# Result rows added to a residual by accumulating DMAs instead of loads, VectorE sums and identity products

## The chip, the cores and the metric

One core of a Trainium2 chip. The metric is the time of one execution on the device, in microseconds (us).

## The reference

Two layers over 512 tokens of width 1024, in float32. Layer 0 mixes tokens by sparse attention, layer 1 by gated linear attention (GLA); both have memory heads beside. Every layer ends with a mixture of 32 experts, of which each token uses two, and two layer norms:

```python
x = layer_norm(ALPHA * x + mixed, ln1_g[i], ln1_b[i])
ffn = hier_moe(x, ...)          # two experts per token, weighted and summed
x = layer_norm(ALPHA * x + ffn, ln2_g[i], ln2_b[i])
```

The change touches the last line: the residual `ALPHA * x` plus the rows that the experts gave, then the norm.

## The kernel before

The 512 tokens lie in four row tiles of 128 rows by 1024 columns, `xb[0]` to `xb[3]`. After the mixer the kernel gathers each expert's tokens (at most 64) and works through the experts in nine groups (`GROUPS`, L1069): seven of four experts and two of two. `moe` (L1191) computes for each group the hidden products (`hidden`, L1096, matmuls at L1103), turns the result (`turned`, L1110) and multiplies by the output weights (L1266), two experts at a time in the two halves of the partitions.

Where the results go depends on the group. Groups 0 to 6 (28 experts) scale their rows into `ys` (L1274) and scatter them to a buffer `Y` in HBM (L1282, an indirect DMA on POOL). `Y` has two halves of 512 rows: a token's row from its first expert is in the first half, that from its second in the second. Both halves are cleared beforehand. The last two groups (experts 28 to 31) are local: their rows are split into a high and a low part `yh`, `yl` (L1270, L1271) and brought to their tokens by products with a one-hot matrix `sp` (L1257). `spread` holds these triples, one for each of the two pairs.

The weights stream in through one DMA queue, issued by SP in a planned order (`load_weights`, L1073, issue at L1055). They go to blocks of an arena in SBUF: `Arena.get` takes the least recently freed place, and a load waits until the former readers of that place are done. Pieces are of 2048, 1536, 1024 or 512 columns, as room is found. Behind layer 0's weights the weights of the GLA layer follow (`split_later`, L309, issue at L312, split by L295 on ScalarE and L296 on VectorE).

At the start of the last group `read_back` (L1355) takes four arena blocks `yb` and issues four loads of `Y` on SP, 1 MB each: row tile i of both halves. The engines' order from there on is the order of the code (`in_order`, L259). `add_first` (L1365) adds the first half of tiles 0 and 1 to the residual on VectorE. `combine` (L1369) ends the layer:

- `part(i, n, early)` brings tile i together in two PSUM tiles of 512 columns. For the first pair (n = 0) it begins with products of `yb` and the identity matrix (L1386): for tiles 0 and 1 of the second half alone, for tiles 2 and 3 of both halves. Then come the one-hot products of `yh` and `yl` (L1388).
- `add(i)` adds PSUM to the residual and forms the sums for the mean (L1395, L1399); ScalarE squares (L1401) and takes the root (L1402).
- `norm(i)` scales and shifts on VectorE (L1407 to L1409).
- `done(i, x)` stores the tile. In layer 1 this is the output (L1743), in layer 0 the store to `x2d` (L1749) and the transposes for the GLA layer's input (`fill`, L1434, L1439).

```python
part(0, 0, True)
part(1, 0, True)
for i in range(NT):
    part(i, 1, False)
    add(i)
    if i + 2 < NT:
        part(i + 2, 0, True)
    if i:
        norm(i - 1)
```

The PSUM pools `mm` and `sc` have two buffers each, so two row tiles are under way at a time. Then the GLA layer begins with its projection (`in_proj`, L558, products at L340 to L342).

Of the kernel before, what the change touches and what calls it, by code (L numbers as in the profile page):

```python
# [10 lines left out]
F32 = mybir.dt.float32  # L11
# [4 lines left out]
OP = mybir.AluOpType  # L16
AX = mybir.AxisListType

P = 128
S = 512  # L20
NT = S // P
D = 1024
# [206 lines left out]
class Trunk:  # L229
# [961 lines left out]
    def moe(self, layer, xb, Y, done):  # L1191


        nc, wk, ar = self.nc, self.wk, self.ar
        NQ = NE // QE
        W = QE * CAP
        xs = [b.v(D) for b in self.xs.blocks]
        xe = [b.v(KD // 2, W)[:, k] for b in self.xe.blocks for k in range(KD // 2)]
        scat, spread, held = [], [], []
        place = {}  # L1200
        oh, ins = self.one_hot(0)
        self.fetch(self.slot_tokens(oh), xs)
        ovf = self.overflow_count()
        with self.tc.issue_after(ins.ins):
            self.routing_rows()
        then = self.slot_tokens(self.one_hot(1)[0])
        self.overflow(layer, Y, ovf)
        order = self.pe_order()
        order.__enter__()
        self.features(xs, xe)  # L1210
        self.fetch(then, xs)
        for g, experts in enumerate(self.GROUPS):
            q, n = experts[0] // QE, len(experts)
            last = g == len(self.GROUPS) - 1
            turns = experts[-1] % QE == QE - 1 and q + 1 < NQ
            if g == NQ - 4:
                self.load_norms(layer)
            if last:
                self.read_back(Y)
                tail = self.in_order((mybir.EngineType.PE, mybir.EngineType.DVE, mybir.EngineType.Activation))  # L1220
                tail.__enter__()
            sas = []
            for s, e in enumerate(experts):
                blocks, rows = self.loaded.pop((layer, e, 0))
                sas.append(self.hidden(xe, e % QE, rows.__getitem__))
                for blk in blocks:
                    blk.free()
                if not last:
                    self.prefetch(layer, *((2 * D,) if g in (NQ - 3, NQ - 2) else ()))
                if g == 0 and s in (1, 2):  # L1230
                    place[s - 1] = self.places(s - 1, self.one_hot(s - 1)[0])
            if turns:
                self.features(xs, xe)
            aT = self.turned(sas)
            if turns and q + 2 < NQ:
                oh, _ = self.one_hot(q + 2)
                place[q + 2] = self.places(q + 2, oh)
                self.fetch(place[q + 2][0], xs)
            if g == NQ - 3:
                self.residual(xb, self.spread_norm(0, ALPHA))  # L1240
            if g == NQ - 2:
                self.gain = self.spread_norm(2, 1.0)
                self.rows.free()
            if last:
                self.xe.free()
                self.xs.free()
            _, token, wt, row = place[q]
            for s in range(0, n, 2):
                j = experts[s] % QE // 2
                ws = [self.loaded.pop((layer, e, 1)) for e in experts[s:s + 2]]  # L1250
                local = q == NQ - 1
                if local:
                    yb = (ar.get(D), ar.get(D))
                    yh, yl = (b.v(D, dt=F32R) for b in yb)
                    ohb = ar.get(S)
                    sp = ohb.v(S, dt=F32R)
                    nc.vector.tensor_scalar(sp, self.c("iota"), token[:, j:j + 1], None, op0=OP.is_equal)  # L1257
                    if last:
                        self.add_first(xb, 0)
                else:  # L1260
                    ys = wk.tile([P, D], F32, name="ys", tag="ys")
                for c in range(2):
                    y = self.pv([P, 512])
                    for f in range(2):
                        for h in range(2):
                            nc.tensor.matmul(y[h * CAP:(h + 1) * CAP, :], aT[:, s + h, f * CAP:(f + 1) * CAP],  # L1266
                                             ws[h][1][2 * f + c], start=(f == 0), stop=(f == 1))
                    cs = slice(c * 512, (c + 1) * 512)
                    if local:
                        nc.scalar.activation(yh[:, cs], y, AF.Copy, scale=wt[:, j:j + 1])  # L1270
                        nc.vector.scalar_tensor_tensor(yl[:, cs], y, wt[:, j:j + 1], yh[:, cs].bitcast(F32),  # L1271
                                                       op0=OP.mult, op1=OP.subtract)
                    else:
                        nc.scalar.activation(ys[:, cs], y, AF.Copy, scale=wt[:, j:j + 1])  # L1274
                for blocks, _ in ws:
                    for blk in blocks:
                        blk.free()
                if local:
                    spread.append((sp, yh, yl))
                    held.extend((ohb, *yb))  # L1280
                    continue
                st = nc.gpsimd.indirect_dma_start(  # L1282
                    out=Y, out_offset=bass.IndirectOffsetOnAxis(ap=row[:, j:j + 1], axis=0),
                    in_=ys, in_offset=None, bounds_check=2 * S - 1, oob_is_err=False)
                for b in scat:
                    self.tc.declare_no_dep(st.ins, b.ins, reason="rows of other slots")
                scat.append(st)
            if not last:
                self.prefetch(layer, *{NQ - 5: (D,), NQ - 4: (2 * D,), NQ - 3: (2 * D,), NQ - 2: (D, D, S)}.get(g, ()))
        self.add_first(xb, 1)  # L1290
        self.combine(xb, spread, done)
        tail.__exit__(None, None, None)
        order.__exit__(None, None, None)
        for b in held:
            b.free()
# [56 lines left out]
                out=Y, out_offset=bass.IndirectOffsetOnAxis(ap=idx[:, 0:1], axis=0),  # L1352
                in_=ys[:CAP], in_offset=None, bounds_check=2 * S - 1, oob_is_err=False)

    def read_back(self, Y):  # L1355

        yv = Y.rearrange("(r i p) f -> p r i f", r=2, p=P)
        self.yb = [self.ar.get(2 * D) for _ in range(NT)]
        for i in range(NT):
            self.nc.sync.dma_start(self.yb[i].v(2, D), yv[:, :, i, :])  # L1360


    EARLY = 2

    def add_first(self, hb, i):  # L1365
        x = hb[i].v(D)
        self.nc.vector.tensor_add(x, x, self.yb[i].v(2, D)[:, 0, :])

    def combine(self, hb, spread, done):  # L1369


        nc, ar, sm = self.nc, self.ar, self.sm
        g, b = (self.gain.v(2, D)[:, j] for j in range(2))
        sqb = ar.get(D)
        st, acc = {}, {}
        last = len(spread) - 1

        def part(i, n, early):

            oh, yh, yl = spread[n]  # L1380
            for c in range(2):
                cs = slice(c * 512, (c + 1) * 512)
                if early:
                    ps = acc[i, c] = (self.mm if c else self.sc)([P, 512])
                    for r in range(int(i < self.EARLY), 2):
                        nc.tensor.matmul(ps, self.ident, self.yb[i].v(2, D)[:, r, cs], start=(r == int(i < self.EARLY)), stop=False)  # L1386
                for y in (yh, yl):
                    nc.tensor.matmul(acc[i, c], oh[:, i * P:(i + 1) * P], y[:, cs], start=False, stop=not early and y is yl)  # L1388

        def add(i):  # L1390
            x = hb[i].v(D)
            s = sm.tile([P, 2], F32, name="csum")
            for c in range(2):
                cs = slice(c * 512, (c + 1) * 512)
                nc.vector.scalar_tensor_tensor(x[:, cs], acc[i, c], 1.0, x[:, cs], op0=OP.mult, op1=OP.add,  # L1395
                                               accum_out=s[:, c:c + 1])
            self.yb[i].free()
            nm = sm.tile([P, 1], F32, name="cmean")
            nc.vector.tensor_scalar(nm, s[:, 0:1], s[:, 1:2], -1.0 / D, op0=OP.add, op1=OP.mult)  # L1399
            sq = sm.tile([P, 1], F32, name="csq")  # L1400
            nc.scalar.activation(sqb.v(D), x, AF.Square, bias=nm, accum_out=sq)  # L1401
            nc.scalar.activation(sq, sq, AF.Sqrt, bias=self.eps[:, 0:1], scale=1.0 / D)  # L1402
            st[i] = x, nm, sq

        def norm(i):
# [3 lines left out]
            nc.vector.scalar_tensor_tensor(x, x, sq, b, op0=OP.mult, op1=OP.add)  # L1409
# [5 lines that stand above are left out]
# [394 lines left out]
```

## Time and profile before

| | us |
|---|---|
| median of 3 runs | 1210.11 |
| lowest, highest | 1205.82, 1212.65 |
| the profiled execution's own time | 1212.06 |
| its span in the profile | 1210.3 |
| TensorE busy | 1105.9 |
| VectorE busy | 591.2 |
| ScalarE busy | 398.5 |
| POOL busy | 178.8 |

Times in the rows are from the start of the span. The stages of layer 0 reach to about 660 us, the last 270 us are the MoE stage of layer 1. A busy share says where an engine works, not what ends last; for that there are the chain of waits, which is followed back from the last instruction, and the timeline, which gives in brackets how long an engine was idle before an instruction and what ended it. PEclk is the granted clock of TensorE as a share of full speed. "HBM" rows and GB/s are those of the core's 16 DMA engines together.

### The profile page before, as it was taken

To read this page: it belongs to the slowest core of one execution; us is meant where nothing else is said; L and a number is where in the kernel's file an instruction comes from. 1 tells how busy PE (TensorE), PEld (TensorE's weight loads), DVE (VectorE), ACT (ScalarE), POOL (GpSimd) and SP (SyncE) were. 2 spreads that over 40 slices of the span, in tenths; PEclk is the share of its full clock that TensorE was granted. 3 is DMA by queue.
4 is the path that set the end of the run, shared out by engine and by line. 5 is a ranking of instruction groups with operands and counts; after the bars stand their busy time and mean duration, and the time that the engine had idled before them with its cause. 6 is when DMAs were issued, how large, how long until landed. Compare 5 with 4: busy or idle time off the path is not lost. (4 is left out here: it accounts for less than half of the span.)

```text
span 1210.3 us, 20344 instructions
## 1 busy us (share of the span) xinstructions
PE 1105.9 (91%) x7864; PEld 799.5 (66%) x7864; DVE 591.2 (49%) x1601; ACT 398.5 (33%) x853; POOL 178.8 (15%) x179
## 2 busy tenths in 40 slices
PE   7999999999998899888988999899896999888985
PEld 7866887767697656444444778899896666444442
DVE  6778894555647422114116745992737322114125
ACT  6421343556512222112215534453501222112212
POOL 0425201000002021111000000553001111111000
PEclk9988899999998899998899999899997999998988
DMA  9033410341577699999997202137196899999992
GB/s 320 27 105 109 131 40 14 101 145 32 189 289 270 253 395 419 422 366 384 396 407 257 79 22 80 41 117 267 65 413 243 317 400 397 368 368 392 408 410 109
DMA packets 101509, 289.35 MB, mean 239 GB/s; under 512 B 13948, under 2 KB 43021, under 8 KB 89762
## 3 DMA queue, kind: packets, MB, share of 16 engines
q1 hardware_dynamic: 88704, 257.42, 56.4%
q0 software_dynamic: 9792, 20.00, 4.5%
q10 hardware_dynamic: 2914, 10.61, 2.2%
q8 instruction: 63, 1.03, 0.4%
q14 instruction: 36, 0.29, 0.1%
HBM read 272.19 MB, written 31.46 MB: 251 GB/s over the span
## 5 line engine op out<-in xcount | busy, mean ns | idle before, releaser
L1103 PE MATMUL mm<-blk,blk 128*64 128x256 f32 x2048 | 246.8, 391 | 30.9 <-DMA blk<-in_w 28.9
L340 PE MATMUL mm<-blk,blk 128*128 128x256 f32 (+2 forms) x800 | 262.7, 329 | 4.6 <-ACT blk L467 3.6
L341 PE MATMUL mm<-blk,blk 128*128 128x256 f32 (+2 forms) x800 | 256.3, 320 | 2.1 <-DVE blk L296 2.1
L342 PE MATMUL mm<-blk,blk 128*128 128x256 f32 (+2 forms) x800 | 255.8, 320 | 0.0
L1103 PEld LDWEIGHTS mm<-blk,blk 128*64 128x64 f32 x2048 | 149.9, 141 | 127.9 <-DMA blk<-in_w 43.0
L340 PEld LDWEIGHTS mm<-blk,blk 128*128 128x128 f32 x800 | 154.8, 194 | 25.7 <-issue 16.5
L1107 DVE TENSOR_TENSOR sa<-sa,mm 128x128 f32<-128x128 f32 x64 | 18.3, 287 | 304.9 <-ACT sa L1106 304.9
L341 PEld LDWEIGHTS mm<-blk,blk 128*128 128x128 f32 x800 | 155.1, 194 | 9.7 <-issue 7.2
L342 PEld LDWEIGHTS mm<-blk,blk 128*128 128x128 f32 x800 | 154.7, 193 | 7.9 <-issue 7.9
L1266 PE MATMUL pv<-blk,aT 128*64 128x512 f32 x512 | 129.7, 638 | 5.4 <-DMA blk<-in_w 2.5
L296 DVE TENSOR_TENSOR blk<-blk,blk 128x768 fp32r<-128x768 f32 (+3 forms) x104 | 106.8, 1041 | 37.3 <-ACT blk L295 37.1
L295 ACT ACTIVATE blk<-blk 128x768 fp32r<-128x768 f32 (+3 forms) x104 | 84.6, 835 | 73.2 <-DMA blk<-in_dsa_w_in 18.2
L1106 ACT ACTIVATE sa<-mm 128x128 f32<-128x128 f32 x64 | 17.7, 277 | 246.5 <-PE mm L1103 246.5
L1266 PEld LDWEIGHTS pv<-blk,aT 128*64 128x64 f32 x512 | 40.0, 146 | 85.4 <-issue 61.9
L1170 POOL DMA_INDIRECT blk<-x1d,at x32 | 34.1, 1065 | 303.0 <-DVE at L1136 232.0
L467 ACT ACTIVATE blk<-tr 128x256 f32<-128x256 f32 (+5 forms) x148 | 57.3, 404 | 53.8 <-PE tr L463 50.2
L1274 ACT ACTIVATE ys<-pv,wts 128x512 f32<-128x512 f32 x56 | 38.5, 687 | 81.1 <-PE pv L1266 56.0
L463 PE MATMUL tr<-cpack,blk 128*128 128x128 f32 x292 | 50.6, 285 | 6.2 <-DVE blk L1439 2.4
L463 PEld LDWEIGHTS tr<-cpack,blk 128*128 128x128 f32 x292 | 34.0, 143 | 19.0 <-issue 7.8
L545 PE MATMUL pv<-blk,blk 128*64 128x128 f32 x368 | 45.3, 289 | 0.3 <-ACT blk L467 0.2
L456 POOL TENSOR_TENSOR rope<-rope,rope 128x384 f32<-128x384 f32 (+2 forms) x28 | 26.1, 933 | 126.8 <-DVE rope L455 112.1
L1282 POOL DMA_INDIRECT Y<-ys,at x28 | 28.3, 1011 | 99.5 <-ACT ys L1274 96.4
(289 smaller groups left out, 1421.4 us busy)
## 6 DMA issues: line engine op xcount, KB each, us to landing
blk<-in_w SPq DMA_DIRECT2D x91, 1024.0 KB
blk<-in_w SPq DMA_DIRECT2D x112, 512.0 KB
blk<-in_w SPq DMA_DIRECT2D x147, 256.0 KB
blk<-in_dsa_w_in SPq DMA_DIRECT2D x24, 384.0 KB
blk<-in_gla_w_in SPq DMA_DIRECT2D x24, 384.0 KB
blk<-in_w SPq DMA_DIRECT2D x11, 768.0 KB
Y<-blk ACTq DMA_DIRECT2D x8, 1024.0 KB
blk<-in_w_out SPq DMA_DIRECT2D x16, 512.0 KB
```

The lines of the kernel that those rows point to most:

```text
L295: self.nc.scalar.activation(hi, raw, AF.Copy)
L296: (eng or self.nc.vector).tensor_sub(lo, raw, hi.bitcast(F32))
L340: self.nc.tensor.matmul(ps, ah, bh, start=(k == 0), stop=False)
L341: self.nc.tensor.matmul(ps, ah, bl, start=False, stop=False)
L342: self.nc.tensor.matmul(ps, al, bh, start=False, stop=(k == KD - 1))
L463: self.nc.tensor.transpose(t[:s.shape[-1], j, :], s, self.ident)
L467: self.nc.scalar.activation(dst, src, AF.Copy)
L545: nc.tensor.matmul(o[s * HD:(s + 1) * HD, i * P:(i + 1) * P], vcol(j, s), pts[s][:, j, :], start=(j == 0), stop=(j == nk - 1))
L1103: nc.tensor.matmul(h[c * CAP:(c + 1) * CAP, 0:256], xe[k][:, e4 * CAP:(e4 + 1) * CAP], w[:, c * 256:(c + 1) * 256], start=(k == 0), stop=( ...
L1170: self.nc.gpsimd.indirect_dma_start(out=xs[j], out_offset=None, in_=self.x1d, in_offset=bass.IndirectOffsetOnAxis(ap=at[:, j:j + 1], axis= ...
L1266: nc.tensor.matmul(y[h * CAP:(h + 1) * CAP, :], aT[:, s + h, f * CAP:(f + 1) * CAP], ws[h][1][2 * f + c], start=(f == 0), stop=(f == 1))
L1274: nc.scalar.activation(ys[:, cs], y, AF.Copy, scale=wt[:, j:j + 1])
```

## The change

The four loads of `Y`, `add_first` and the identity products are gone, and the buffers `yb` with them. In their place `read_back` issues eight DMAs on POOL per layer, each of which adds 128 rows of one half of `Y` (512 KB) to the residual tile in SBUF: for tiles 0 and 1 the first halves, then the second halves, then the same for tiles 2 and 3. Ahead of them stands a copy of one column on POOL, which reads the last piece of the output weights of the last group's first expert (`then`), so that POOL waits for that weight. POOL is now one of the engines that keep the order of the code in the tail. `add(i)` is unchanged and reads the residual when both sums have landed.

```diff
@@ moe
             if last:
-                self.read_back(Y)
-                tail = self.in_order((mybir.EngineType.PE, mybir.EngineType.DVE, mybir.EngineType.Activation))
+                tail = self.in_order((mybir.EngineType.PE, mybir.EngineType.DVE, mybir.EngineType.Activation,
+                                      mybir.EngineType.Pool))
                 tail.__enter__()
+                self.read_back(Y, xb, self.loaded[layer, experts[0], 1][1][-1])
...
-                    if last:
-                        self.add_first(xb, 0)
...
-        self.add_first(xb, 1)
         self.combine(xb, spread, done)
@@ read_back
-    def read_back(self, Y):
+    def read_back(self, Y, hb, then):
+        nc = self.nc
+        nc.gpsimd.tensor_copy(self.sm.tile([P, 1], F32, name="novf"), then[:, 0:1])
         yv = Y.rearrange("(r i p) f -> p r i f", r=2, p=P)
-        self.yb = [self.ar.get(2 * D) for _ in range(NT)]
-        for i in range(NT):
-            self.nc.sync.dma_start(self.yb[i].v(2, D), yv[:, :, i, :])
+        for i0 in range(0, NT, 2):
+            for r in range(2):
+                for i in (i0, i0 + 1):
+                    nc.gpsimd.dma_start(hb[i].v(D), yv[:, r, i, :], accum_op=OP.add)
@@ combine
                 if early:
-                    ps = acc[i, c] = (self.mm if c else self.sc)([P, 512])
-                    for r in range(int(i < self.EARLY), 2):
-                        nc.tensor.matmul(ps, self.ident, self.yb[i].v(2, D)[:, r, cs], start=(r == int(i < self.EARLY)), stop=False)
+                    acc[i, c] = (self.mm if c else self.sc)([P, 512])
                 for y in (yh, yl):
-                    nc.tensor.matmul(acc[i, c], oh[:, i * P:(i + 1) * P], y[:, cs], start=False, stop=not early and y is yl)
+                    nc.tensor.matmul(acc[i, c], oh[:, i * P:(i + 1) * P], y[:, cs],
+                                     start=early and y is yh, stop=not early and y is yl)
...
-            self.yb[i].free()
```

The order of POOL's instructions at the end of layer 1, before: the scatters to `Y`, then the end of the program.

```order
L1282 DMA Y<-ys,at 1024x1024 x4
L1796 UNCONDITIONAL_BRANCH
```

Now (blk_8406 to blk_8412 are the four residual tiles, blk_11178 the piece of weights):

```order
L1281 DMA Y<-ys,at 1024x1024 x4
L1356 COPY novf<-blk_11178 128x1
L1361 DMA blk_8406<-Y 128x1024
L1361 DMA blk_8408<-Y 128x1024
L1361 DMA blk_8406<-Y 128x1024
L1361 DMA blk_8408<-Y 128x1024
L1361 DMA blk_8410<-Y 128x1024
L1361 DMA blk_8412<-Y 128x1024
L1361 DMA blk_8410<-Y 128x1024
L1361 DMA blk_8412<-Y 128x1024
L1787 UNCONDITIONAL_BRANCH
```

The eight sums stand behind the copy, and the second sum into a tile two places behind its first.

TensorE in `combine` of layer 1, from the last one-hot products of tile 0 to those of tile 2, before (sc and mm are the two PSUM tiles, blk_11389 is the loaded `Y` of tile 2, cpack the identity):

```order
L1388 MATMUL mm<-blk_11438,blk_11440 128x512
L1388 MATMUL mm<-blk_11439,blk_11440 128x512
L1386 MATMUL sc<-blk_11389,cpack 128x512 x2
L1388 MATMUL sc<-blk_11367,blk_11369 128x512
L1388 MATMUL sc<-blk_11368,blk_11369 128x512
L1386 MATMUL mm<-blk_11389,cpack 128x512 x2
L1388 MATMUL mm<-blk_11367,blk_11369 128x512
L1388 MATMUL mm<-blk_11368,blk_11369 128x512
```

Now:

```order
L1379 MATMUL mm<-blk_11382,blk_11384 128x512
L1379 MATMUL mm<-blk_11383,blk_11384 128x512
L1379 MATMUL sc<-blk_11309,blk_11311 128x512
L1379 MATMUL sc<-blk_11310,blk_11311 128x512
L1379 MATMUL mm<-blk_11309,blk_11311 128x512
L1379 MATMUL mm<-blk_11310,blk_11311 128x512
```

The rows with the identity are gone, the others stand in the same order.

SP between the weights of layer 0 and those of the GLA layer, as a difference:

```order
-L1360 DMA blk_6233<-Y 128x2x1024
-L1360 DMA blk_6235<-Y 128x2x1024
-L1360 DMA blk_6237<-Y 128x2x1024
-L1360 DMA blk_6239<-Y 128x2x1024
```

The loads of the GLA layer's weights (L312) now follow directly on the last expert's. In layer 1 the places of many weight pieces differ too: SP issues 123 loads of 512 columns (256 KB) for expert weights in place of 147, and more of 2048 columns.

## Rows read from the trace of the kernel before

**Rows 1.** The page: TensorE's busy time, and DMA in 40 slices of the span.
```profile
PE 1105.9 (91%) x7864; PEld 799.5 (66%) x7864; DVE 591.2 (49%) x1601; ACT 398.5 (33%) x853; POOL 178.8 (15%) x179
...
DMA  9033410341577699999997202137196899999992
```

**Rows 2.** The chain that ended last, layer 1: start us, us, engine, tile, line.
```profile
1158.97 5.82 PE pv L1266 x13
...
1177.70 1.06 PE sc L1386 x2
...
1183.67 0.71 DVE blk L1395 x2
...
1184.42 1.98 PE sc L1386 x4
...
1186.87 1.72 PE mm L1386 x4
...
1189.55 0.71 DVE blk L1395 x2
...
1195.43 1.32 DVE blk L1395 x4
...
1196.78 0.21 DVE cmean L1399
1196.99 1.19 DVE blk L1407
...
1198.29 1.28 DVE blk L1409
...
1204.94 1.29 DVE blk L1409
```

**Rows 3.** Windows at the end: length, busy us by engine, PEclk, DMA share, GB/s.
```profile
1172.00:1176.00 4.00, 3.05 (x15) 1.10 (x15) 1.10 (x3) 0.28 (x1) 0.00 (x0) 1.00 1.03 411
1176.00:1180.00 4.00, 4.00 (x15) 1.62 (x12) 3.02 (x4) 1.38 (x2) 0.00 (x0) 1.00 1.02 409
...
1184.00:1188.00 4.00, 3.66 (x11) 1.81 (x11) 1.20 (x5) 2.71 (x4) 0.00 (x0) 1.00 0.00 0
```

**Rows 4.** Timeline, end of layer 0: third add, first projection product; [idle before <- releaser].
```profile
656.09 0.69 DVE L1395 SCALAR_TENSOR_TENSOR blk<-sc,blk 128x512 f32<-128x512 f32 x1
...
661.93 0.40 PE L340 MATMUL mm<-blk,blk 128*128 128x272 f32 x1 [3.63 <-ACT blk L467]
```

**Rows 5.** Windows: start of layer 1's MoE stage; both MoE streams in full flow.
```profile
936.00:942.00 6.00, 4.54 (x21) 3.27 (x23) 1.75 (x4) 4.28 (x6) 1.98 (x2) 0.50 0.11 17
...
460.00:490.00 30.00, 29.95 (x246) 18.57 (x244) 6.47 (x22) 6.08 (x14) 4.04 (x4) 1.00 1.02 419
990.00:1020.00 30.00, 29.94 (x238) 17.83 (x236) 6.04 (x21) 7.44 (x15) 6.31 (x7) 1.00 1.03 401
```

**Rows 6.** Line L1367, the sums on VectorE: ns min/median/max, first and last start.
```profile
L1367 DVE TENSOR_TENSOR blk<-blk,blk x4: 1219/1224/1226, 638.3 to 1179.5; 128x1024 f32<-128x1024 f32 x4
```

**Rows 7.** Timeline, layer 0: output products of the last pair waiting for weights.
```profile
634.37 0.20 PEld L1266 LDWEIGHTS pv<-blk,aT 128*64 128x64 f32 x4 [0.96 <-DMA blk<-in_w]
635.02 0.41 PEld L1266 LDWEIGHTS pv<-blk,aT 128*64 128x64 f32 x4 [0.45 <-DMA blk<-in_w]
```

**Rows 8.** Line L892, the stores of x1d on POOL's queue, 512 KB each.
```profile
L892 POOL DMA_DIRECT2D x1d<-blk x8: 531/542/749, 366.2 to 916.2; - x8
...
DMA to landing us min/median/max: 6.8/7.7/8.7
```

**Rows 9.** Row gathers on that queue: all; the second of a pair; GB/s, 926:936 in 40 slices.
```profile
DMA to landing us min/median/max: 3.8/9.4/11.2
...
928.74 1.02 POOL L1170 DMA_INDIRECT blk<-x1d,at  x1 [0.30 <-DVE dn L967]
...
GB/s 0 0 0 0 0 0 0 0 0 0 0 0 131 115 147 295 295 213 197 246 164 295 213 131 164 98 33 49 16 16 0 0 0 0 0 0 0 0 0 0
```

**Rows 10.** The page, DMA issues by line and size: the smallest pieces of expert weights.
```profile
blk<-in_w SPq DMA_DIRECT2D x147, 256.0 KB
```

More of the change, by code (lines that the diff above doesn't have):

```diff
@@ L1353, in overflow @@
                 in_=ys[:CAP], in_offset=None, bounds_check=2 * S - 1, oob_is_err=False)
-    def read_back(self, Y):
+    def read_back(self, Y, hb, then):
+        nc = self.nc
+        nc.gpsimd.tensor_copy(self.sm.tile([P, 1], F32, name="novf"), then[:, 0:1])
         yv = Y.rearrange("(r i p) f -> p r i f", r=2, p=P)
-        self.yb = [self.ar.get(2 * D) for _ in range(NT)]
-        for i in range(NT):
-            self.nc.sync.dma_start(self.yb[i].v(2, D), yv[:, :, i, :])
[L1363 to L1367, printed above, removed]
+        for i0 in range(0, NT, 2):
+            for r in range(2):
+                for i in (i0, i0 + 1):
+                    nc.gpsimd.dma_start(hb[i].v(D), yv[:, r, i, :], accum_op=OP.add)
     def combine(self, hb, spread, done):
```

## The prediction

> **What bounds the kernel now.** I read the page first: one core, TensorE busy nearly everywhere, and the DMA row at 9 tenths through both MoE stages (slices 14 to 21 and 29 to 39) [rows 1]. Then the chain of waits, from its end [rows 2]. It shows the last stretch as four pieces: weights arriving until 1158.9, then output products of the last pair but one and the last pair's hidden and output products until 1177.7, products with the identity and with the one-hot matrix until 1183.7, and then a rhythm of 5.9 us per row tile (DVE adds at 1183.67, 1189.55, 1195.43) that closes with DVE alone: from the third add to the end of the last instruction 1204.94 + 1.29 - 1195.43 = 10.8 us. In that rhythm TensorE holds the chain: 1.98 + 1.72 us of identity products per tile against 0.9 us of one-hot products. So the edited lines lie on the path at the end. The windows around that place show the DMA queue: full at 411 GB/s through 1176, empty after 1184 [rows 3]. The four Y loads (4.2 MB, 10.3 us at 409 GB/s) are the last of it, so the weights were all in at about 1173.7, and those of the first expert of the last pair, 1.05 MB earlier, at 1171.1.
>
> In layer 0 the same tail is followed by the GLA layer. TensorE waits there for the copy of a transposed row tile and starts the projection at 661.93 [rows 4]. That copy's DVE half stands behind the third add (656.09), 5.8 us before. The delay of a third add in layer 0 therefore moves the projection one to one, and from there the program follows: at 936 to 942 the queue moves 17 GB/s, that is, nothing is left to prefetch, so the weight stream of layer 1 also starts when the MoE stage does [rows 5].
>
> **What goes.** Twelve identity products per layer, two instructions each at 0.43 us of issue (the chain's 1.98 us for four): 24 x 0.43 = 10.3 us of TensorE per layer, 8 of the 12 inside the rhythm (1.98 + 1.72 us for each of tiles 2 and 3) and 4 before the first add. Two sums of 1.22 us on VectorE per layer [rows 6], which hid beside TensorE but also delayed the scaling of the last pair. Four loads per layer on SP, and 32 KB per partition of their buffers.
>
> **What comes.** Eight transfers of 512 KB per layer on POOL's software queue, in the order first halves of tiles 0 and 1, second halves of 0 and 1, then the same for 2 and 3. A second half waits for its first half to land, since both write the same tile, and POOL takes them in order. They start behind a copy on POOL that waits for the last piece of the first expert's output weights. That gate opens at 1171.1 + 0.4 = 1171.5 in layer 1. In layer 0 the products of that pair wait until 634.37 and 635.02 for pieces of the second expert's weights [rows 7]; the first of these, 0.5 MB, is 1.3 us of the queue, so the first expert's were in and the gate opens at 633.0. Nothing else queues behind it on POOL in layer 1; in layer 0 there are four column fills of one element, used much later.
>
> Without identity products TensorE needs only 0.9 us per tile and part, so VectorE is left with, for each tile, 1.32 + 0.21 us of add and mean and 1.19 + 1.28 of norm [rows 2]: 16.0 us for four tiles. The first add could come at 1177.7 + 1.5 (my estimate for scaling the last pair) + 0.9 = 1180.1, the end at 1196.1 or a little later: **at most 10 us** less than 1206.2. In layer 0 I take 5 at most, since weight pieces whose loads wait for the first pair's last products stand between on VectorE.
>
> **When do the sums land?** The trace of before has no accumulating transfer. Nearest is the same instruction on the same queue with the same size: the four stores of x1d per layer, 0.54 us each on POOL and 6.8 to 8.7 us from issue to landing, median 7.7 [rows 8]. They ran beside weight loads. Far from it, but on the same queue, are the row gathers: 3.8 us at the least, and a pair of them in an idle queue, issued at 927.18 and 928.74, has its bytes in at about 933.3, 4.6 us after the second issue [rows 9]. The third tile needs three landings in a row: second transfer (first half of tile 1), then fifth (first half of tile 2, issued right behind the fourth), then seventh. With two issues of 0.54 between, the third add can start at gate + 1.1 + 3 x landing. I take 7.7, the row of the same instruction: the extra read of the destination makes it longer, the emptier queue shorter, and I know neither.
>
> - Layer 1: 1171.5 + 1.1 + 23.1 = 1195.7 against 1195.43: +0.3.
> - Layer 0: 633.0 + 24.2 = 657.2 against 656.09: +1.1, and 1 us for sharing the queue with GLA weights, whose loads now come right behind the last expert's: +2.1.
> - Layout: without the Y buffers, weights of layer 1 fall into larger pieces (123 loads of 256 KB instead of 147 by SP's order) [rows 10]. Layer 0, with 33 of the 147, streams at 419 GB/s where layer 1, with 114, streams at 401 [rows 5]; a third of the way at most, over 220 us, is 3 us. I take 1, since where each load waits changes too.
>
> Sum +1.4 us on the profiled execution's own 1212.06 us, which stands 1.95 above the median of the three runs, 1210.11. I set the prediction against the median: **1212 us**. So ten microseconds of TensorE work leave the path and three landings take their place.
>
> The Trainium skill, "DMA: Bandwidth & Descriptors", section "Anatomy of one DMA — SWDGE (gpsimd) path", fits a transfer on this queue as 2.0 us plus bytes over 436 GB/s, an estimate of 3.2 us for 512 KB; the stores' 6.8 us at the least speak against it here, and by it the time would be that of the first rival.
>
> **Rivals.**
> - *Landings like the gathers'.* With 4.6 us the third add could be at 1186.4 and 647.9. Layer 1 gains 9.0, layer 0 its 5, layout 1: **1195 us**. For it: from 1174 on the queue of layer 1 is empty, and the target is the core's memory as with the gathers. Against: the stores' lowest value. Between the two, each microsecond of landing is 3 us per layer.
> - *The sum doubles the transfer* (the case slower than before). Each transfer must read the old tile as well as Y. 512 KB more at 405 GB/s is 1.3 us; the two links of the chain that stand behind another transfer pay twice. 2.6 + 2.6 + 1.3 = 6.5 us per layer on top of the forecast: **1225 us**. Place: the third add waits for DMA in both layers while TensorE and VectorE idle. It decides from a landing of 8.7 us (+3 us per layer over the forecast). For it: a second source must come from somewhere. Against: the stores' 7.7 already contains waiting beside weight loads that layer 1 lacks.
> - *Layout decides*: weight loads of layer 1 wait at other frees. The row of layer 1 shows no more than a rate [rows 5]; that of layer 0 is 4% above it, 9 us over 220, and I allow half of it either way, 5 us.
>
> The Trainium skill, "Collectives: The Full Stack", section "The bandwidth ceiling: the fold count and why AG ≠ RS ≠ AR", says a reduction in the DMA engines runs at half the rate of a copy because it reads two sources. No row of before shows it; by it the time is that of the second rival.
>
> **How the numbers follow.** Forecast 0.45, gather-like 0.22, doubled 0.27, layout 0.06. The measurement can tell about 0.5%, 6 us, from no change: faster is under 1204, slower over 1216. The forecast's own range, landings of 6.8 to 8.7 us, is 1206 to 1218; it gives 0.04 to faster and 0.05 to slower, layout 0.02 to each. Faster 0.28, same 0.38, slower 0.34. The range 1199 to 1226 takes in the forecast, most of the doubled case, and the gather-like one where landings are only partly shorter; it leaves out 0.1 on each side.
>
> **What would show it.** Right: no identity product, POOL's copy near 1171 plus the shift of layer 0, issue to landing of the sums near 7.7 us, the third adds waiting for DMA, and first adds earlier than before, by some microseconds. The doubled case shows bytes of the sums at half the loads' rate and the third add over 3 us later, both layers alike. The gather-like case shows adds and norms on VectorE without idle time between. The forecast is wrong if the gate opens much later than 1171.5, if the layers differ by more than 5 us, or if the time between the two tails, MoE stream of layer 1 included, changes by more than 5 us.

## The result and the profile after

The changed kernel takes **1220.69 us** (median of 11 runs, 1213.27 to 1227.51) against 1210.94 us for the kernel before on the same chip: a ratio of 1.0092, 95% interval 1.0062 to 1.0121. It is slower by 0.9%, inside the predicted range (1199 to 1226) and above the own range of the likeliest case (1206 to 1218). The profiled execution took 1225.17 us. In the table of experiments below, the ratios leave out two executions in a slower state, one of kernel 7 (3498.62 us) and one of kernel 9 (1218.82 us), which the medians there include.

The page of the changed kernel (busy us and instructions; queues: packets, MB, share of 16 engines; the chain that ended last, by engine):

```profile
span 1223.4 us, 20232 instructions
...
PE 1088.9 (89%) x7816; PEld 789.0 (64%) x7816; DVE 586.9 (48%) x1597; ACT 399.5 (33%) x853; POOL 190.1 (16%) x197
...
q1 hardware_dynamic: 83216, 249.03, 53.6%
q0 software_dynamic: 12096, 28.39, 8.2%
...
DMA 11%; PE 9%; DVE 1%; issue 1%; POOL 0%; ACT 0%; SPq 0%; DVEq 0%; POOLq 0%
```

The same lines of the page before, for the queues and the chain:

```profile
q1 hardware_dynamic: 88704, 257.42, 56.4%
q0 software_dynamic: 9792, 20.00, 4.5%
...
PE 12%; DMA 8%; DVE 2%; issue 0%; SPq 0%; ACT 0%; DVEq 0%
```

TensorE lost 17 us of work against [rows 1] and the kernel got longer. The queues say where the price is: 8.39 MB moved from q1 to q0. On q1 they took 56.4% of 1210.3 less 53.6% of 1223.4, 26.9 us of all sixteen engines; on q0 they take 8.2% of 1223.4 less 4.5% of 1210.3, 45.9 us. That is 2.9 us for each of the 16 transfers.

The chain that ended last, end of layer 1 (start us, us, what), answers to [rows 2]:

```profile
1173.50 7.72 DMA blk<-in_w
1181.22 2.05 issue
...
1192.45 9.06 DMA blk<-Y
...
1204.27 8.26 DMA blk<-Y
1212.66 1.32 DVE blk L1387 x4
...
1218.10 1.28 DVE blk L1400
```

Before, the chain ran at 5.9 us per tile, with TensorE holding it; now it runs through last weights, gate and landings. The timeline of layer 1 shows each step (the copy that is the gate, the issues of the sums, the adds; in brackets the idle time before and what ended it):

```profile
1182.86 0.42 DVE L1116 COPY aT<-pv 128x256 f32<-128x256 f32 x1 [0.42 <-PE pv L1114]
...
1183.27 0.45 POOL L1356 COPY novf<-blk 128x1 f32<-128x1 f32 x1 [21.55 <-issue]
1183.81 1.90 POOL L1361 DMA_DIRECT2D blk<-Y  x2
1189.42 0.87 POOL L1361 DMA_DIRECT2D blk<-Y  x1 [3.70 <-DMA blk<-Y]
1191.91 2.65 POOL L1361 DMA_DIRECT2D blk<-Y  x3 [1.62 <-DMA blk<-Y]
1201.80 0.87 POOL L1361 DMA_DIRECT2D blk<-Y  x1 [7.24 <-DMA blk<-Y]
...
1194.68 0.69 DVE L1387 SCALAR_TENSOR_TENSOR blk<-sc,blk 128x512 f32<-128x512 f32 x1 [4.70 <-DMA blk<-Y]
...
1207.46 0.69 DVE L1387 SCALAR_TENSOR_TENSOR blk<-sc,blk 128x512 f32<-128x512 f32 x1 [4.77 <-DMA blk<-Y]
...
1212.66 0.69 DVE L1387 SCALAR_TENSOR_TENSOR blk<-sc,blk 128x512 f32<-128x512 f32 x1 [1.05 <-DMA blk<-Y]
...
631.93 0.42 POOL L1356 COPY novf<-blk 128x1 f32<-128x1 f32 x1 [10.86 <-DMA blk<-in_w]
...
662.78 0.69 DVE L1387 SCALAR_TENSOR_TENSOR blk<-sc,blk 128x512 f32<-128x512 f32 x1 [4.73 <-DMA blk<-Y]
```

From gate to third add it is 1207.46 - 1183.27 = 24.2 us in layer 1 and 662.78 - 631.93 = 30.9 us in layer 0 (last two rows). Executions drift by several us before either tail, so tails are best compared from one fixed instruction: `aT`, the copy of the last pair's turned hidden rows (first row above for layer 1). Its other rows, layer 0 of the changed kernel first, then the kernel before:

```profile
631.49 0.42 DVE L1116 COPY aT<-pv 128x256 f32<-128x256 f32 x1 [0.42 <-PE pv L1114]
...
632.74 0.43 DVE L1116 COPY aT<-pv 128x256 f32<-128x256 f32 x1 [0.42 <-PE pv L1114]
...
1173.56 0.42 DVE L1116 COPY aT<-pv 128x256 f32<-128x256 f32 x1 [0.42 <-PE pv L1114]
```

The third add stands 21.9 us behind it before and 24.6 after in layer 1, 23.4 and 31.3 in layer 0.

The windows (length, busy us by engine, PEclk, DMA share, GB/s) show what the queue does meanwhile, in layer 0 and layer 1:

```profile
640.00:650.00 10.00, 0.67 (x2) 0.56 (x3) 1.43 (x5) 1.68 (x2) 3.71 (x7) 0.63 1.06 256
...
1190.00:1200.00 10.00, 5.92 (x18) 3.70 (x16) 3.03 (x10) 2.82 (x4) 2.93 (x4) 0.83 1.04 190
```

In layer 1 the sums alone fill the DMA engines (share 1.04) and move **190 GB/s**; the loads of before moved 410 at the same share [rows 3]. In layer 0 TensorE is nearly idle for ten microseconds, and GLA weights share the queue.

Put together, the profiled execution is 13.1 us longer, where the medians stand 9.75 us apart; so some microseconds of the shifts belong to these two executions and not to the change. The steps are read as the shift of the same instruction between the two traces. The last pair of layer 0 came 1.3 us earlier (scatter before the change acts). The third add of layer 0 lost 7.9 against it, so it stands 6.7 later (662.78 for 656.09). The last store of x1d stands 11.5 later (927.7 for the 916.2 of [rows 8]): 265.0 us behind the third add for 260.1. These 4.8 us are not shown to come from the change: run 5, below, whose layer 0 is that of the kernel before, takes 264.2 us for the same stretch, and run 8, with the same layer 0, 262.3. Third add and last store in run 5:

```profile
651.77 0.69 DVE L1405 SCALAR_TENSOR_TENSOR blk<-sc,blk 128x512 f32<-128x512 f32 x1
...
915.97 0.53 POOL L892 DMA_DIRECT2D x1d<-blk  x1 [1.95 <-DVE lg L837]
```

The `aT` copy of layer 1 is 9.3 later, so it gained 2.2 against that store. The end is 13.1 later: that tail lost 3.9 against `aT`.

### The profile page after: what moved, and what is told of

Same layout as the page of the kernel before. It is cut to its first block, busy times and chain, and to the rows that moved or that the text cites. A ratio compares the mean times of both kernels' runs of the same rounds, so it can differ in the third digit from the quotient of the medians.

```text
span 1223.4 us, 20232 instructions
## 1 busy us (share of the span) xinstructions
PE 1088.9 (89%) x7816; PEld 789.0 (64%) x7816; DVE 586.9 (48%) x1597; ACT 399.5 (33%) x853; POOL 190.1 (16%) x197
## 3 DMA queue, kind: packets, MB, share of 16 engines
q1 hardware_dynamic: 83216, 249.03, 53.6%
## 5 line engine op out<-in xcount | busy, mean ns | idle before, releaser
L463 PEld LDWEIGHTS tr<-cpack,blk 128*128 128x128 f32 x292 | 34.2, 144 | 22.4 <-issue 8.2
```

What stands on the lines that cost most here:

```text
L463: self.nc.tensor.transpose(t[:s.shape[-1], j, :], s, self.ident)
```

## Experiments

Two theories stood at the start. **A**: dependent landings follow one another, and the order of issue makes the time. **B**: a sum costs the DMA engines twice a copy, and the bytes make the time. Beside them: C, the gate comes late; D, GLA weights in layer 0; E, the layout of layer 1's weights. All results (ratio to the kernel before, 95% interval; third add and end in us behind `aT`, from the profiled execution):

| kernel | median us | ratio | third add, layer 0 | third add, layer 1 | end, layer 1 |
|---|---|---|---|---|---|
| before | - | 1 | 23.4 | 21.9 | 32.7 |
| changed | 1220.69 | 1.0092 (1.0062 to 1.0121) | 31.3 | 24.6 | 36.5 |
| 1 all first halves first | 1216.80 | 1.0072 (1.0044 to 1.0100) | 31.6 | 24.3 | 35.1 |
| 2 no gate | 1234.03 | 1.0209 (1.0161 to 1.0256) | 24.2 | 21.2 | 31.9 |
| 3 plain copies | 1199.66 | 0.9944 (0.9906 to 0.9983) | 23.5 | 17.3 | 28.1 |
| 4 hybrid | 1216.31 | 1.0076 (1.0049 to 1.0104) | 32.6 | 24.9 | 35.7 |
| 5 layer 1 alone | 1212.91 | 1.0032 (1.0003 to 1.0060) | 23.4 | 23.1 | 33.8 |
| 6 layer 0 alone | 1214.14 | 1.0060 (1.0026 to 1.0093) | 31.0 | 23.4 | 34.2 |
| 7 hybrid, later gate | 1208.66 | 0.9993 (0.9962 to 1.0025) | 24.8 | 20.4 | 31.2 |
| 8 the same, layer 1 alone | 1209.00 | 0.9987 (0.9959 to 1.0016) | 23.3 | 20.4 | 31.1 |
| 9 four sums on GpSimd | 1204.55 | 0.9963 (0.9938 to 0.9988) | 20.6 | 20.3 | 31.0 |
| 10 no read-back | 1196.85 | 0.9911 (0.9882 to 0.9939) | 15.8 | 14.7 | 25.5 |
| 11 two sums on GpSimd | 1203.87 | 0.9946 (0.9915 to 0.9978) | 20.8 | 19.9 | 30.7 |

**1. Another order.**

```diff
-for i0 in range(0, NT, 2):
-    for r in range(2):
-        for i in (i0, i0 + 1):
+for r in range(2):
+    for i in range(NT):
```

> The changed kernel with the eight sums of each layer in another order: the first halves of all four tiles, then the second halves, so that a second half is issued four transfers behind the one it waits for. Theory A (the third add waits for three dependent landings): only one landing is still waited for in a row, the third add comes at about gate + 1.1 + 2 x 7.7 = 16.5 us instead of 24.2 (layer 1) and 30.9 (layer 0), and the kernel gains 6 to 8 us per layer: about 1206 to 1209 us. Theory B (the transfers themselves take the time, 2.6 us each, one behind another): the seventh transfer ends at gate + 7 x 2.6 + some 4 us of latency = 22 us whatever the order, so layer 1 gains 2 us, layer 0 up to 8: about 1212 to 1219 us.

Its timeline on POOL in layer 1:

```profile
1176.32 0.47 POOL L1359 COPY novf<-blk 128x1 f32<-128x1 f32 x1 [21.49 <-issue]
1176.87 3.69 POOL L1361 DMA_DIRECT2D blk<-Y  x4
1182.92 0.87 POOL L1361 DMA_DIRECT2D blk<-Y  x1 [2.36 <-DMA blk<-Y]
1185.45 0.87 POOL L1361 DMA_DIRECT2D blk<-Y  x1 [1.67 <-DMA blk<-Y]
1187.96 0.87 POOL L1361 DMA_DIRECT2D blk<-Y  x1 [1.64 <-DMA blk<-Y]
1190.20 0.87 POOL L1361 DMA_DIRECT2D blk<-Y  x1 [1.38 <-DMA blk<-Y]
```

Four sums stand in the queue, and still each next one is released only 2.2 to 2.5 us behind the last: that is the pace of the transfers, not of a wait. Tile 0 is complete only behind the fifth transfer, so the first add comes 16.5 us behind `aT` instead of 11.8. The tail won 1.4 us at its end, the kernel nothing that the intervals tell apart. A asked for 6 to 8 us per layer and falls. B's range holds, but the third adds gained only 0.3 us in layer 1, where it expected 2, and nothing in layer 0.

**2. No gate.**

```diff
-nc.gpsimd.tensor_copy(self.sm.tile([P, 1], F32, name="novf"), then[:, 0:1])
```

> The changed kernel without the copy on POOL that holds the sums back until the first expert's output weights are in; the sums start when the last scattered rows are in Y, some 20 us earlier (608 and 1161 us were the last scatters' issues). Theory C (the gate makes the sums late): the third add no longer waits for DMA, and each layer gains 5 to 10 us: about 1200 to 1210 us. Theory B (the bytes of the sums cost the DMA engines 21 us per layer wherever they lie): the last pair's weights come up to 15 us later, and what the tail gains the products before it lose: within 5 us of the changed kernel's 1221 us.

No add waits for a sum any more, and from `aT` to the end layer 1 takes 31.9 us instead of 36.5, yet the kernel is slower than the changed one. The windows of layer 1:

```profile
1165.00:1175.00 10.00, 8.81 (x59) 3.92 (x55) 1.36 (x4) 1.24 (x3) 1.90 (x2) 1.00 1.02 411
...
1185.00:1195.00 10.00, 5.66 (x24) 2.44 (x24) 0.00 (x0) 0.00 (x0) 1.84 (x3) 0.50 1.06 252
```

The engines are full in both, but with sums among the weights they move 252 GB/s instead of 411, and the last pair's weights come late: `aT` stands at 1198.47 against 1182.86. B's cost is paid elsewhere, and it is 13 us where B said "within 5 us"; the kernel gains nothing of what C promised. The gate was the better choice.

**3. Plain copies.** Same queue, order and gate; the residual and the first choice's rows are left out of the result.

```diff
-nc.gpsimd.dma_start(hb[i].v(D), yv[:, r, i, :], accum_op=OP.add)
+nc.gpsimd.dma_start(hb[i].v(D), yv[:, r, i, :])
```

> The changed kernel with the same eight transfers, queue, order and gate, but as plain copies that overwrite the tile: the residual and the first choice's rows are left out of the result. Theory B (reading the old tile costs as much again): a 4 KB packet falls from some 320 ns to about 145 ns, a transfer's engine time from 2.6 to 1.3 us, and the third add comes 4 to 7 us earlier in each layer: about 1206 to 1213 us. Theory A (what a landing costs is the queue's fixed time, not the sum): landings stay at 7 us and above, and the time stays within 4 us of the changed kernel's 1221 us.

Lines of the transfer in the changed kernel (duration on POOL, ns min/median/max; landing from issue):

```profile
L1361 POOL DMA_DIRECT2D blk<-Y x16: 848/913/1558, 632.5 to 1204.3; - x16
...
DMA to landing us min/median/max: 5.1/7.6/12.5
```

and with plain copies, with the queue's line of the page:

```profile
L1361 POOL DMA_DIRECT2D blk<-Y x16: 537/540/592, 622.4 to 1176.0; - x16
...
DMA to landing us min/median/max: 3.5/5.8/8.4
...
q0 software_dynamic: 12096, 28.34, 6.6%
```

6.6% of 1193.5 us less the 54.5 us of before leaves 24.3 us for the 16 transfers, 1.5 us each: the sum costs 1.9 times the copy. Between the two ratios lie 1.5%, some 18 us. This shows B: the same transfers without the sum beat the kernel before, with it they lose. The gain is more than B expected (1206 to 1213 us): the third adds come 7.8 and 7.3 us earlier than in the changed kernel, for 4 to 7. What inside the transfer takes the added time, the reading of the old tile or the addition, no run here separates.

**4. Hybrid.** Tiles 0 and 1 as before, tiles 2 and 3 by sums.

```diff
+self.yb = {i: self.ar.get(2 * D) for i in (0, 1)}
+for i, b in self.yb.items():
+    nc.sync.dma_start(b.v(2, D), yv[:, :, i, :])
-for i0 in range(0, NT, 2):
...
+for i, r in ((2, 0), (3, 0), (2, 1), (3, 1)):
+    nc.gpsimd.dma_start(hb[i].v(D), yv[:, r, i, :], accum_op=OP.add)
```

> Tiles 0 and 1 as in the kernel before (rows loaded, first half added on VectorE, second by identity products), tiles 2 and 3 by accumulating transfers in the order 2, 3 first halves, 2, 3 second halves, behind the same gate. Half of the sums' bytes, and no identity product inside the rhythm of the adds. Theory A: the third add stands behind two landings, gate + 1.1 + 2 x 7.7 = 16.5 us; layer 1 gains 5 us over the kernel before, layer 0 up to 5: about 1201 to 1207 us. Theory B: three transfers of 2.6 us and a latency of 4, gate + 12: then VectorE holds the rhythm and both layers gain 7 to 9 us: about 1194 to 1198 us. Rival: four landings beside the loads of the next layer take as long as eight, and the time stays at 1210 us or above.

Both theories missed, and the time is the rival's; its reason, the next layer's loads, can hold in layer 0 alone. What TensorE waited for, layer 1:

```profile
PE sc L1393 <- DMA blk<-Y: 3.7, 1, 3.7
```

L1393 is the identity product of the first tiles: their loads now share the engines with the sums and come late, the first add stands 18.2 us behind `aT` instead of 10.1. Two streams on full engines delayed each other here, the urgent one too.

**5, 6. One layer alone.** In the other layer loads, sums on VectorE and identity products as before.

```diff
+SUMS = {0: [], 1: ALL}      # 5;  6: {0: ALL, 1: []}
+LOADS = {0: [0, 1, 2, 3], 1: []}      # 5;  6: {0: [], 1: [0, 1, 2, 3]}
```

> The change in layer 1 alone: layer 0 loads the rows and multiplies them with the identity as before. From the two traces, the stretch from the last pair's turned hidden copy to the end of layer 1 grew from 32.7 to 36.5 us, and the weight stream of layer 1 got some 2 us shorter. Theory B+D (the transfers' own time of 2.6 us each in layer 1; in layer 0 that and the GLA weights beside them): +3 to +5 us over the kernel before, about 1211 to 1215 us. Rival E (the layout of layer 1's weight buffers decides): +8 us and more, or a gain.

> The change in layer 0 alone. From the two traces, the third add of layer 0 stood 23.4 us behind the turned hidden copy before and 31.3 us after, and work up to the last store of x1d came 11.5 us later. Theory B+D: +7 to +11 us over the kernel before, less some 2 us that the weight stream of layer 1 gains from the layout: about 1215 to 1220 us. Rival: the two layers cost the same (the forecast's third add was 0.3 and 2.1 us late): +4 to +5 us.

Run 5 falls inside its range, run 6 0.9 us below its own, and they add up: 0.32% and 0.60% against 0.92% for both. The intervals of the two overlap; that the layers do not cost the same is read from the third adds: 1.2 us late in layer 1, 7.6 in layer 0. What differs between the layers is what else is on the queue: nothing in layer 1, GLA weights in layer 0.

Layout as the main cause (E) is out, though not by run 5, whose weight loads have the sizes of the kernel before (147 of 256 KB). Runs 3 and 10 have those of the changed kernel (123) and are faster than the kernel before, and run 6, which has them too, costs 7.3 us with a third add 7.6 us late. Run 6 also shows what layer 1's tail, with the code of before, looks like in that layout: third add and end stand 23.4 and 34.2 us behind `aT` instead of 21.9 and 32.7. Of the 3.9 us that the tail of the changed kernel lost against `aT`, 1.5 are therefore there without any sum in layer 1.

**7, 8. Hybrid with a later gate**, in both layers and in layer 1 alone.

```diff
-nc.gpsimd.tensor_copy(self.sm.tile([P, 1], F32, name="novf"), then[:, 0:1])
+nc.gpsimd.tensor_copy(self.sm.tile([P, 1], F32, name="novf"), self.yb[1].v(2, D)[:, 1, 0:1])
```

> The hybrid (tiles 0 and 1 loaded, tiles 2 and 3 by accumulating transfers), with the copy on POOL waiting for the loaded rows of tile 1 instead of the weights, so that no sum shares the queue with weights or with those loads. Theory B: tile 0's first add is where it was before (10 us behind the turned hidden copy), then tile 2's third transfer ends 3 x 2.6 + 2 us behind the loads, so the third add comes 3 to 4 us earlier than before in layer 1; in layer 0 the GLA weights share the queue, and it comes 0 to 5 us later: about 1207 to 1213 us. Theory A: two landings of 7.7 behind the loads, third add 1 to 3 us later than before in both layers: 1213 to 1217 us.

> The same hybrid in layer 1 alone, where nothing else is left for the queue; layer 0 as before. Theory B: the third add of layer 1 comes 3 to 4 us earlier than before, and so does the end: about 1206 to 1208 us. Theory A: 1 to 3 us later: 1211 to 1214 us. A time below the kernel before would make this the version that beats both.

With the sums behind the loads, the first hybrid's loss is gone. Layer 1's third add comes 1.5 us earlier than before, not 3 to 4, and kernel 8 misses its 1206 to 1208 us by 1; layer 0's comes 1.5 later in kernel 7. Its adds in layer 1 (kernel 8; `aT` at 1173.06):

```profile
1187.17 0.69 DVE L1405 SCALAR_TENSOR_TENSOR blk<-sc,blk 128x512 f32<-128x512 f32 x1 [1.04 <-PE sc L1397]
1193.42 0.69 DVE L1405 SCALAR_TENSOR_TENSOR blk<-sc,blk 128x512 f32<-128x512 f32 x1 [2.09 <-DMA blk<-Y]
```

Even four sums in an otherwise empty queue still hold the third add for 2.1 us. Neither interval leaves 1: a tie with the kernel before, half as many sums and no loss.

**9. Most of the relief of TensorE without the sums' traffic.** The kernel before; tiles 2 and 3 lose their identity products (8 of the 12 per layer), GpSimd adds their rows from the loaded blocks.

```diff
+for i in (2, 3):
+    for r in range(2):
+        nc.gpsimd.tensor_add(xb[i].v(D), xb[i].v(D), self.yb[i].v(2, D)[:, r, :])
...
-for r in range(int(i < self.EARLY), 2):
+for r in range(int(i < self.EARLY), 2 if i < 2 else 0):
```

> The kernel before with the identity products of tiles 2 and 3 alone taken away, and their rows added by four sums on GpSimd per layer (some 2.7 us each by the row of 1.375 us for 512 columns) in place of them: the relief of TensorE of the changed kernel without its traffic. Theory B (the change loses by the transfers' time, not by what it takes off TensorE): the rhythm falls from 5.9 to some 4 us a tile, the third add comes 3 to 4 us earlier in each layer, and so does what follows: about 1201 to 1205 us. Rival (the identity products were not what held the tail, or GpSimd's sums slow VectorE): 1207 to 1211 us.

It beats both kernels: 0.9963 (0.9938 to 0.9988), as B said. So the identity products did hold the tail, and taking them off the path is worth time if the sums do not go to the DMA engines. The third add came 2.8 and 1.6 us earlier, less than the 3 to 4 expected. VectorE and GpSimd in layer 1:

```profile
1173.26 10.49 POOL L1293 TENSOR_TENSOR blk<-blk,blk 128x1024 f32<-128x1024 f32 x4 [33.63 <-DMA blk<-Y]
...
1177.19 0.69 DVE L1398 SCALAR_TENSOR_TENSOR blk<-sc,blk 128x512 f32<-128x512 f32 x1 [1.02 <-PE sc L1391]
1178.66 2.89 DVE L1410 SCALAR_TENSOR_TENSOR blk<-blk,cmean,blk 128x1024 f32<-128x1024 f32 x1
1181.66 3.17 DVE L1412 SCALAR_TENSOR_TENSOR blk<-blk,csq,blk 128x1024 f32<-128x1024 f32 x1
...
1186.22 1.27 DVE L1410 SCALAR_TENSOR_TENSOR blk<-blk,cmean,blk 128x1024 f32<-128x1024 f32 x1
```

The norm's two instructions take 2.89 and 3.17 us while GpSimd adds and 1.27 afterwards; the add with one operand in PSUM keeps its 0.69.

**10. No read-back**: the rows of experts 0 to 27 are left out of the result, with loads, sums and identity products.

```diff
-self.read_back(Y, xb, self.loaded[layer, experts[0], 1][1][-1])
```

> The changed kernel without the read-back: no copy, no sums, so the rows of all experts but the last quarter's local ones are left out of the result. It prices the cap of the prediction: with no load, no sum and no identity product the tail of layer 1 has at most 10 us to give and that of layer 0 at most 5, about 1195 us. Rival: the last pair's products hold the tail, and less than 5 us come in all: 1205 us.

0.9911, some 11 us: the most that any way of adding these rows could win. The tails show 7.6 us at layer 0's third add and 7.2 at layer 1's end, against the 5 and 10 that the prediction took as caps.

**11. Two sums on GpSimd**, the first halves of tiles 2 and 3, the second halves by identity products.

```diff
+for i in (2, 3):
+    nc.gpsimd.tensor_add(xb[i].v(D), xb[i].v(D), self.yb[i].v(2, D)[:, 0, :])
...
-for r in range(int(i < self.EARLY), 2):
+for r in range(1, 2):
```

> As the kernel with four sums on GpSimd, but only the first halves of tiles 2 and 3 there (two sums of 2.4 us per layer), the second halves by identity products. In the run with four sums the norms of tile 0 on VectorE took 2.89 and 3.17 us while GpSimd added, 1.28 us later, and the third add came 7.6 us behind the second. Theory (VectorE and GpSimd hold each other up while both run): with GpSimd done by some 14 us behind the turned hidden copy, no norm is over 1.5 us, and the third add comes at 17 to 18.5 us behind it in layer 1 instead of 20.3: about 1200 to 1204 us. Rival (the identity products left in the rhythm, 1.0 us a tile, hold the third add again): at 20 us and the time of the kernel with four sums, 1204 to 1207 us.

The norms are back to 1.28 us, the third add at 19.9 us missed its 17 to 18.5 and stands where the rival put it, at 20. The timeline shows why:

```profile
1171.66 0.69 DVE L1397 SCALAR_TENSOR_TENSOR blk<-sc,blk 128x512 f32<-128x512 f32 x1 [2.37 <-PE sc L1390]
...
1175.82 0.69 DVE L1397 SCALAR_TENSOR_TENSOR blk<-sc,blk 128x512 f32<-128x512 f32 x1 [2.60 <-PE sc L1390]
...
1177.30 1.28 DVE L1409 SCALAR_TENSOR_TENSOR blk<-blk,cmean,blk 128x1024 f32<-128x1024 f32 x1
```

The first two adds still wait for TensorE; from the second on VectorE works without waiting, 4.1 to 4.3 us a tile. It is the fastest median of the variants that compute the whole result, 0.9946 (0.9915 to 0.9978), though not told apart from kernel 9.

## Why the prediction was right and wrong

- **What bounds the tail** held. Identity products were on the path (runs 9 and 11), and landings took their place, as forecast: the first and third adds wait for DMA in both layers. Their price was a little high: 48 instructions fewer took 17.0 us off TensorE, 0.35 us each, where the prediction has 0.43 (that is four in the 1.72 us of [rows 2], not in the 1.98).
- **Gate + 1.1 + 3 x landing** gave 24.2 us, and layer 1 measured 24.2. That it fits to the tenth is luck: the three links behind the 1.1 us and one more issue took 7.5, 9.3 and 5.7 us (second transfer to the release of the fourth, fifth to the release of the seventh, seventh to the third add), so the sum was met and its even parts were not. The median of all sums, 7.6, is close to the 7.7 of [rows 8], but the stores ran beside weights and these sums in an otherwise empty queue, at half the rate of the loads.
- **"1 us for sharing the queue with GLA weights" in layer 0** is the term that failed most. Gate to third add took 30.9 us, not 25.2: 5.7 us too little, the largest single share of what the forecast missed; run 6 repeats it with 30.6. The same three links took 11.0, 10.4 and 7.7 us there. Engines at 1.06 of share serve both streams; layer 1, with nothing beside the sums, is the control.
- **"That gate opens at 1171.5 in layer 1"** came out as meant, "near 1171 plus the shift of layer 0": 1183.27 less the 11.5 us by which the last store of x1d is later is 1171.8. Against `aT` the gate is 2.5 us later than forecast (0.4 us behind it, which is 1174.0 in the trace before), because `aT` gained 2.2 us and the weights 0.2: by the semaphore events of the two traces the last weight load lands at 1174.31 before and at 1185.63 after, 11.3 later. The 2.05 us of "issue" in the chain in front of the copy are a wait that the page does not link: the same events have another weight load landing 0.1 us before the copy starts. In layer 0 the gate, read from real waits [rows 7], was right within 0.2 us.
- **First adds "earlier than before, by some microseconds"** failed: behind `aT` they come at 11.8 instead of 10.1 us in layer 1, and at 17.1 instead of 11.6 in layer 0. Two landings in a row took longer than the sums and identity products that they replaced.
- **The rest of the tail** was taken as unchanged, 10.8 us. It is 1219.38 - 1207.46 = 11.9: the last sum lands 5.2 us behind the third add, where VectorE alone would be ready in 4.1.
- **"From there the program follows"** is not refuted. The GLA layer took 4.8 us longer in the profiled execution, but runs 5 and 8, with an unchanged layer 0, took 4.1 and 2.2 us longer than the trace of before too, and the waits of TensorE there are 13.3 us in the changed kernel, 9.4 before and 12.3 in run 5.
- **Layout**, -1: the right sign, as far as it can be told. From the last store of x1d to `aT` of layer 1 it takes 254.8 to 258.0 us in the traces with the weight loads of before (before, 5, 8, 9, 11) and 251.8 to 255.2 in those with the changed kernel's (changed, 1, 3, 6, 10), 2.4 less on average. In the changed kernel the last weights landed only 0.2 us sooner behind that store, and the tail gave part of the gain back (run 6).
- **The rivals.** "The sum doubles the transfer" is what the runs show: 190 GB/s for 410, 2.9 us for 1.5, its own sign in the list of what would show it. That the second read is the reason stays argued. Its other sign, both layers alike, did not come. It priced both layers at 6.5 us more than the forecast; by runs 5 and 6 layer 1 cost 3.9 and layer 0 7.3 us more than before (0.32% and 0.60%, with intervals of 0.03 to 0.60% and 0.26 to 0.93%). Its 1225 us lay 4 above the result, the forecast's 1212 nearly 9 below. The argument against it, that the stores' 7.7 us contain waiting which layer 1 lacks, bounded the wrong thing: the eight transfers in a row went at the pace of their rate, and no landing of a single plain transfer holds that. The Trainium skill, "Collectives: The Full Stack", section "The bandwidth ceiling: the fold count and why AG ≠ RS ≠ AR", has the reduction of a ring collective at half a copy's rate because of its second source; the trace agrees with the half rate, 190 against 410 GB/s, for an accumulating DMA on one core, and shows nothing of the reason. "Landings like the gathers'" falls: no sum landed under 5.1 us.
- **By its own list** two points went against the forecast: the layers differ by more than 5 us (third add 7.9 and 2.7 late), and the first adds came later. The time lies in the stated range because that was made to take in most of the doubled case, not because the likeliest case came in. A chance of 0.34 for slower was too small for a mechanism with a rule behind it and only an indirect row against it.

## What to carry to other kernels

An accumulating DMA is not a free adder: here it took the DMA engines 1.9 times a copy, so moving a sum from compute to DMA trades compute for traffic. It won in none of these runs; the best was a tie, with half the sums and, in layer 1, an otherwise empty queue (runs 7 and 8). Price a burst of dependent transfers by its rate and by what else is on the queue, not by the landing of one. Before moving work off a bounding engine, list the idle ones: most of the same relief on GpSimd, without the sums' traffic, beat both kernels.

## What was not expected of the hardware

- An accumulating DMA of 512 KB holds POOL for 0.91 us per issue (median), the plain copy of the same shape 0.54.
- GpSimd's sums slowed VectorE's norms from 1.28 to 2.89 and 3.17 us, and not the adds that read PSUM (0.69). The Trainium skill, "SBUF — State Buffer", section "Who interferes with whom", has the two engines share a pair of ports under an exclusive lock. The trace fits that: the norms read two tiles from SBUF, the adds one. With GpSimd's two sums moved out of the norms' way (run 11), the norms take 1.28 again.
- TensorE's granted clock was 0.63 on average in the window of layer 0 in which it waited for sums and was busy for 0.67 of 10 us, so for part of it the lower of its two levels (1.2 of 2.4 GHz). In run 2 it was at 0.50, the lower level, while TensorE worked through late weights (5.66 of 10 us busy). What either cost was not measured by itself.
